# Group 0's output projection in one pass over its weights instead of two

## The chip, the cores and the metric

The kernel runs on one core of a Trainium2 chip. Its engines are TensorE (PE, with its weight loads shown as PEld), VectorE (DVE), ScalarE (ACT), GpSimd (POOL) and SyncE (SP), which issues nearly all of the DMAs. The metric is the device time of one execution in microseconds; lower is better. The time before is 1418.04 us, the median of 3 runs (1415.65 to 1418.85).

## The reference, cut to what matters

One layer of a streaming encoder in fp32, over a group of 1024 new frames and one of 32 frames that continue a stream. The change lies between the three mixers and the feed-forward network:

```
mod = silu(c) @ w_ada + b_ada
sh1, sc1, g1, sh2, sc2, g2 = split(mod, 6)
h = x * (1 + sc1) + sh1
... = split(h @ w_in)                          # mLSTM, forgetting attention, gMLP -> hm, hf, hg
mix = concatenate([hm, hf, hg]) @ w_o           # (tokens, 1024) @ (1024, 1024): the output projection
x = layer_norm(ALPHA * x + (1 + g1) * mix, ln1_g, ln1_b)
h = x * (1 + sc2) + sh2
y = (silu(h @ w_gate) * (h @ w_up)) @ w_down
x = layer_norm(ALPHA * x + (1 + g2) * y, ln2_g, ln2_b)
```

## The kernel before

**Layout.** Activations are kept transposed, features on the partitions: 1024 features are KT = 8 tiles of 128 rows. The 1056 tokens are two groups, c = 0 with 512 tokens and c = 1 with 544, and each group is cut in two halves, `MM[0] = ((0, 256), (256, 512))` and `MM[1] = ((0, 272), (272, 544))`.

**Precision.** A product of fp32 is made of three faster ones. Each operand is split into a rounded high part, cast by ACT, and the rest, subtracted by DVE: of weights by `weights` (L105 and L106, tiles `raw`, `whi`, `wlo`), of the mix by `wo_mix` (L903 and L904, tiles `ah...` and `al...`). `gemm` then issues three matmuls per feature tile, high by high (L117), high by low (L118), low by high (L119). Three tiles of `raw` and three each of `whi` and `wlo` go round.

**Group 0's output projection** is phase `wo` in the trace, at 388.7 to 439.8 us. The mixers left their output in `dmix` in DRAM, and `wo_mix` loads it by 128x256 pieces into four `tmp` buffers, by feature tiles in the order `KORDER = (2, 3, 4, 5, 0, 1, 6, 7)`. For every m, one of eight tiles of output features, `wo` loads 512 KB of w_o, splits it and makes the product, 24 matmuls for a half of the tokens. Before the change `run` calls `wo` once per half:

```
for cut in MM[0]:
    self.wo(0, st, (cut,), nc.vector)
```

so the weights are read and split twice. Group 1's `wo` (phase `wo` at 916.8 to 966 us) has both halves in one call. Only for m = 0 are the products taken feature tile by feature tile over the halves, so that they can follow the mix as it comes.

**What happens to a product.** It lies in one of three PSUM banks (pool `pg`, tiles `wo_g`). `sublayer_end` adds it to the residual z (L943, DVE), which frees the bank, and keeps the sums that the layer norm wants. To keep the squares small, a pivot is taken off z: after m = 0, `ln_pivot` makes the mean of z's first tile with a matmul (L836, tile `wo_t`), ACT copies it to `pv` (L837), and DVE takes it off that tile (L838). For every later m POOL takes it off z (L938) before the product is added. POOL also sums z (L851, `zs`); ACT squares it (L844, L847) and DVE sums the squares (L853, `qs`). Then `ln1` normalises each half and writes it, split again, to the operand of the feed-forward units (`up`), which follow after four units of keys and queries (`fm`).

**What sets the order.** Each engine runs its instructions in one order, laid down ahead of time by a scheduler with a time model of its own; every wait is on the semaphore of an instruction or a DMA. So an instruction that waits holds up whatever stands behind it on its engine, and a load on SP is issued only when those ahead of it are. The profile's line numbers are those of the kernel before; in the changed one the same lines stand 16 further down from `wo` on (L943 becomes L959, L938 becomes L954).

Of the kernel before, what the change touches and what calls it, by code (L numbers as in the profile page):

```python
# [7 lines left out]
F32 = mybir.dt.float32  # L8
F32R = mybir.dt.float32r
AF = mybir.ActivationFunctionType  # L10
ALU = mybir.AluOpType
# [54 lines left out]
def f(ap):  # L66
    return ap.bitcast(F32)


class Kernel:  # L70
# [820 lines left out]
    def operand(self, c, pool):  # L891

        new = lambda tag, n: self.t(pool, [P, KT * 272], F32R, tag, 1)[:, :KT * n].rearrange("p (k n) -> p k n", k=KT)
        self.hh[c], self.hl[c] = ({a: new(f"{x}{a}", b - a) for a, b in MM[c]} for x in ("ah", "al"))

    def wo_mix(self, c, ks):
        self.phase = f"wo{c}"
        nc = self.nc
        for a, b in MM[c]:
            for k in ks:  # L900
                r = self.t(self.p2, [P, 272], F32, "tmp", 4)[:, :b - a]
                self.load(r, self.dmix[c][:, k, a:b])
                nc.scalar.copy(self.hh[c][a][:, k], r)  # L903
                nc.vector.tensor_tensor(self.hl[c][a][:, k], r, f(self.hh[c][a][:, k]), ALU.subtract)  # L904
# [6 lines left out]
    def wo(self, c, st, cuts, eng, res=None):  # L911
# [6 lines left out]
        for m in range(KT):  # L918
# [5 lines left out]
            if m == 0:  # L924
                for i in range(KT):
                    for p, (a, b) in zip(ps, cuts):
                        self.gemm(p[:, :b - a], w[i:i + 1], slice(0, P), lambda _: hh[a][:, ko[i]],
                                  lambda _: hl[a][:, ko[i]], start=i == 0, stop=i == KT - 1)
            for p, (a, b) in zip(ps, cuts):
                if m:  # L930
                    self.gemm(p[:, :b - a], w, slice(0, P), lambda i: hh[a][:, ko[i]], lambda i: hl[a][:, ko[i]])
                self.sublayer_end(c, z, m, p, "g1", st, a, b)
# [19 lines left out]
    def ln1(self, c, st, a, b):  # L952
# [3 lines left out]
        for k in range(KT):  # L956
# [11 lines left out]
            nc.scalar.copy(hh[:, k], h)  # L968
            nc.vector.tensor_tensor(hl[:, k], h, f(hh[:, k]), ALU.subtract)  # L969
# [29 lines left out]
    def up(self, c, j, act, pool, cuts, w=None):  # L999
# [4 lines left out]
        for a, b in cuts:  # L1004
            ps = []
            for i in range(2):
                p = self.t((self.pg, self.pu)[i], [P, 512], F32, self.utag[i])[:, :b - a]
                self.gemm(p, w[i], slice(0, P), lambda k: hh[a][:, k], lambda k: hl[a][:, k])
# [33 lines left out]
    def sup_operand(self, ks):  # L1042
# [164 lines left out]
    def run(self):  # L1207
# [128 lines left out]
        for cut in MM[0]:  # L1336
            self.wo(0, st, (cut,), nc.vector)
# [211 lines left out]
```

## Time and profile before

| | |
|---|---|
| median of 3 runs | 1418.04 us (1415.65 to 1418.85) |
| profiled execution | 1418.36 us, of which the span from first to last instruction is 1416.6 |
| PE busy | 1364.1 us, 96% of the span, in 10945 matmuls |
| DVE, ACT, POOL busy | 1041.1, 657.7 and 255.8 us |
| moved by DMA | 231.97 MB, mean 164 GB/s |
| group 0's output projection | 384 matmuls, from 388.7 to 439.5 us |

A row of a timeline is start, duration, engine, line, operation, tile written, tiles read and shape; in brackets stands how long the engine was idle ahead of it and who ended that. Grouped rows have a count (x24) and durations in nanoseconds. Two matmuls overlap, so one that takes 0.28 us starts 0.12 after the one ahead of it.

### The profile page before, as it was taken

What the parts mean: (1) busy time and instruction counts of PE and PEld (TensorE: products, weight loads), DVE (VectorE), ACT (ScalarE), POOL (GpSimd) and SP (SyncE); (2) the same over time, 40 slices, a digit from 0 to 9 for tenths busy, and PEclk for the clock granted to TensorE, in tenths of its full rate; (3) what the DMA queues carried; (4) which work ended last, traced back from release to release, by engine and by line L of the source; (5) the groups of instructions that cost most, each with busy time, mean ns of one, the idle gap of its engine ahead of it and who ended that gap; (6) DMA issues with size and microseconds to landing.
All of it is one profiled execution on the core that took longest, in us unless ns stands there. A gap on an engine that the chain in (4) does not pass through costs nothing.

```text
span 1416.6 us, 28810 instructions
## 1 busy us (share of the span) xinstructions
PE 1364.1 (96%) x10945; PEld 1312.5 (93%) x10945; DVE 1041.1 (73%) x2363; ACT 657.7 (46%) x1395; POOL 255.8 (18%) x298
## 2 busy tenths in 40 slices
PE   7999999999999899999999999999999999999996
PEld 4799988999889789999999999999999999999996
DVE  5548645678679678687777765678977988878777
ACT  3313234444446464555555453335663454535354
POOL 0103200043157400000000000364610000000331
PEclk9999999999999999999999999999999999999999
DMA  9664578575754765344334422654586567542321
GB/s 359 246 216 132 172 224 238 174 229 157 224 185 147 185 206 173 99 142 148 111 112 146 90 98 86 179 172 128 177 214 182 159 176 202 155 135 92 118 98 64
DMA packets 135698, 231.97 MB, mean 164 GB/s; under 512 B 22516, under 2 KB 79484, under 8 KB 135560
## 3 DMA queue, kind: packets, MB, share of 16 engines
q1 hardware_dynamic: 130520, 220.56, 49.2%
q0 software_dynamic: 4896, 9.44, 4.4%
q8 instruction: 86, 1.41, 0.4%
q14 instruction: 52, 0.43, 0.1%
q10 hardware_dynamic: 144, 0.14, 0.0%
HBM read 196.19 MB, written 52.76 MB: 176 GB/s over the span
## 4 chain that ended last, share of the span: by engine, by line
PE 76%; DVE 9%; DMA 8%; ACT 3%; issue 2%; SPq 1%; POOL 1%; DVEq 0%; ACTq 0%; POOLq 0%
PE up_g L118 6%; PE up_g L119 5%; PE up_g L117 5%; PE dn_g L117 4%; PE dn_g L118 4%; PE dn_g L119 4%; PE tm_g L282 3%; PE tm_g L283 3%; PE tm_g L284 3%; PE fm_g L117 2%; PE fm_g L119 2%; PE fm_g L118 2%; PE fox_t L732 2%; PE wo_g L117 2%; PE wo_g L118 2%
## 5 line engine op out<-in xcount | busy, mean ns | idle before, releaser
L117 PE MATMUL up_g<-wo_ah,up_whi 128*128 128x256 f32 (+1 forms) x720 | 205.4, 286 | 3.9 <-ACT lna_tmp L964 3.3
L118 PE MATMUL up_g<-wo_al,up_whi 128*128 128x256 f32 (+1 forms) x720 | 207.4, 288 | 0.6 <-DVE wo_al L969 0.6
L119 PE MATMUL up_g<-wo_ah,up_wlo 128*128 128x256 f32 (+1 forms) x720 | 205.9, 286 | 0.0
L117 PEld LDWEIGHTS up_g<-wo_ah,up_whi 128*128 128x128 f32 x720 | 136.6, 190 | 5.4 <-ACT wo_ah L968 3.5
L118 PEld LDWEIGHTS up_g<-wo_al,up_whi 128*128 128x128 f32 x720 | 136.8, 190 | 1.6 <-DVE wo_al L969 0.8
L119 PEld LDWEIGHTS up_g<-wo_ah,up_wlo 128*128 128x128 f32 x720 | 136.8, 190 | 0.4 <-DVE up_wlo L106 0.2
L117 PE MATMUL fm_g<-start_h1h,fm_whi 128*128 128x256 f32 (+2 forms) x344 | 102.1, 302 | 8.4 <-DVE fm_qkl L367 3.6
L283 PE MATMUL tm_g<-tm_wlo,start_h1h 128*128 128x256 f32 (+1 forms) x384 | 110.1, 287 | 0.0
L284 PE MATMUL tm_g<-tm_whi,start_h1l 128*128 128x256 f32 (+1 forms) x384 | 109.8, 287 | 0.0
L282 PE MATMUL tm_g<-tm_whi,start_h1h 128*128 128x256 f32 (+1 forms) x384 | 109.2, 286 | 0.2 <-ACT tm_mixs L633 0.2
L117 PE MATMUL dn_g<-up_acth,dn_whi 128*128 128x256 f32 (+1 forms) x352 | 102.4, 291 | 0.2 <-DVE sup_uv L1116 0.2
L118 PE MATMUL fm_g<-start_h1l,fm_whi 128*128 128x256 f32 (+2 forms) x344 | 101.7, 296 | 0.0
L119 PE MATMUL fm_g<-start_h1h,fm_wlo 128*128 128x256 f32 (+2 forms) x344 | 101.1, 295 | 0.0
L118 PE MATMUL dn_g<-up_actl,dn_whi 128*128 128x256 f32 (+1 forms) x352 | 100.5, 286 | 0.0
L119 PE MATMUL dn_g<-up_acth,dn_wlo 128*128 128x256 f32 (+1 forms) x352 | 100.4, 285 | 0.0
L1087 ACT CAST sup_whi<-sup_raw 128x1024 fp32r<-128x1024 f32 x51 | 52.7, 1047 | 80.7 <-PE dn_u L118 28.1
L735 ACT CAST fox_pth<-fox_t 128x256 fp32r<-128x256 f32 (+3 forms) x144 | 51.1, 373 | 67.5 <-PE fox_t L732 63.0
L117 PEld LDWEIGHTS fm_g<-start_h1h,fm_whi 128*128 128x128 f32 x344 | 65.4, 192 | 14.0 <-DVE fm_qkl L367 4.3
L106 DVE TENSOR_TENSOR up_wlo<-up_raw,up_whi 128x1024 fp32r<-128x1024 f32 x52 | 66.2, 1273 | 16.5 <-ACT up_whi L105 15.7
L1088 DVE TENSOR_TENSOR sup_wlo<-sup_raw,sup_whi 128x1024 fp32r<-128x1024 f32 x51 | 63.1, 1244 | 17.0 <-ACT sup_whi L1087 17.0
L105 ACT CAST up_whi<-up_raw 128x1024 fp32r<-128x1024 f32 x52 | 54.5, 1047 | 45.2 <-PE up_g L118 19.7
L736 DVE TENSOR_TENSOR fox_ptl<-fox_t,fox_pth 128x256 fp32r<-128x256 f32 (+3 forms) x144 | 58.0, 417 | 23.7 <-ACT fox_pth L735 22.4
(575 smaller groups left out, 4676.9 us busy)
## 6 DMA issues: line engine op xcount, KB each, us to landing
up_raw<-w_gu SPq DMA_DIRECT2D x52, 512.0 KB
dn_raw<-w_dn SPq DMA_DIRECT2D x28, 512.0 KB
ada_late<-w_ada SPq DMA_DIRECT2D x24, 512.0 KB
wo_raw<-w_o SPq DMA_DIRECT2D x24, 512.0 KB
sup_raw<-w_gu SPq DMA_DIRECT2D x19, 512.0 KB
start_dp<-w_gu SPq DMA_DIRECT2D x18, 512.0 KB
start_dp<-w_gu POOLq DMA_DIRECT2D x18, 512.0 KB, 7.6
sup_raw<-start_dp SPq DMA_DIRECT2D x17, 512.0 KB
```

The costliest lines, as they stand in the source:

```text
L105: nc.scalar.copy(hi[:, :w], raw[:, :w])
L106: (eng or nc.vector).tensor_tensor(lo[:, :w], raw[:, :w], f(hi[:, :w]), ALU.subtract)
L117: nc.tensor.matmul(ps, hi, xh(k), start=start and k == 0, stop=False)
L118: nc.tensor.matmul(ps, hi, xl(k), start=False, stop=False)
L119: nc.tensor.matmul(ps, lo, xh(k), start=False, stop=stop and k == n - 1)
L282: nc.tensor.matmul(ps[:, :ncol], xh, hi, start=k == 0, stop=False)
L283: nc.tensor.matmul(ps[:, :ncol], xh, lo, start=False, stop=False)
L284: nc.tensor.matmul(ps[:, :ncol], xl, hi, start=False, stop=k == 7)
L735: nc.scalar.copy(ph[:, lo:nq], ps[:, lo:nq])
L736: nc.vector.tensor_tensor(pl[:, lo:nq], ps[:, lo:nq], f(ph[:, lo:nq]), ALU.subtract)
L1087: nc.scalar.copy(h, x)
L1088: tt(l, x, f(h), ALU.subtract)
```

## The change

`wo(0, ...)` is called once with both halves, so each unit of w_o is loaded and split once and serves both. The halves' four operand tiles become two of 8 x 544 columns (`ah` and `al`), with the halves as views, and they are allocated once for the projection and the normalised operand after it. `wo_mix` loads whole feature tiles of 128x512 through the two `sil` buffers, 8 loads in place of 16. The later user of this memory, `sup_operand`, takes its four operands as quarters of the two tiles.

```diff
     def operand(self, c, pool):
+        if c == 0:
+            if 0 not in self.hh:
+                tile = lambda tag: self.t(pool, [P, KT * 544], F32R, tag, 1)[:, :KT * 512].rearrange(
+                    "p (k n) -> p k n", k=KT)
+                self.hh[0], self.hl[0] = ({0: x, 256: x[:, :, 256:]} for x in (tile("ah"), tile("al")))
+            return
...
     def wo_mix(self, c, ks):
         self.phase = f"wo{c}"
         nc = self.nc
+        if c == 0:
+            h, l = self.hh[0][0], self.hl[0][0]
+            for k in ks:
+                r = self.t(self.p2, [P, 544], F32, "sil", 2)[:, :512]
+                self.load(r, self.dmix[0][:, k])
+                nc.scalar.copy(h[:, k], r)
+                nc.vector.tensor_tensor(l[:, k], r, f(h[:, k]), ALU.subtract)
+            return
...
         if not self.T:
-            self.T = [[self.t(self.ph, [P, 2176], F32R, f"{x}{i}", 1).rearrange("p (k n) -> p k n", k=4)
-                       for x in ("ah", "al")] for i in (0, 256)]
+            parts = [self.t(self.ph, [P, KT * 544], F32R, x, 1) for x in ("ah", "al")]
+            self.T = [[x[:, i:i + 2176].rearrange("p (k n) -> p k n", k=4) for x in parts] for i in (0, 2176)]
...
         st = self.ln_begin(nc.gpsimd)
-        for cut in MM[0]:
-            self.wo(0, st, (cut,), nc.vector)
+        self.wo(0, st, MM[0], nc.vector)
         self.operand(0, self.ph)
```

The other lines of the diff only cut the operand's views to the width of a half (`hh[:, k]` becomes `hh[:, k, :b - a]`).

On three engines the order around the projection moves. First SP, from the load of feature 6 to the last of the mix. `dmix_31` is group 0's mix, `raw` a unit of w_o, `dqh`, `dql` and `o_kT` are stores of keys and queries. Before:

```order
L87 DMA wo_tmp_5347<-start_dmix_31_87 128x256
L87 DMA wo_tmp_5351<-start_dmix_31_87 128x256
L91 DMA start_dqh_57<-fm_qkh_5336 128x272
L87 DMA wo_tmp_5355<-start_dmix_31_87 128x256
L87 DMA wo_raw_5562<-w_o 128x1024
L91 DMA start_dql_58<-fm_qkl_5337 128x272
L87 DMA wo_tmp_5359<-start_dmix_31_87 128x256
L91 DMA o_kT<-fm_qkr_5338 64x272
```

Here features 6 and 7 of the first half (5347, 5351) stand together, and those of the second half (5355, 5359) behind them. After:

```order
L87 DMA wo_sil_5321<-start_dmix_31_87 128x512
L91 DMA start_dqh_57<-fm_qkh_5310 128x272
L87 DMA wo_raw_5683<-w_o 128x1024
L91 DMA start_dql_58<-fm_qkl_5311 128x272
L87 DMA wo_sil_5325<-start_dmix_31_87 128x512
L91 DMA o_kT<-fm_qkr_5312 64x272
L87 DMA wo_raw_5751<-w_o 128x1024
L87 DMA wo_raw_5819<-w_o 128x1024
```

Two whole tiles stand where four halves stood, and feature 7 (5325) now stands behind a store of queries and the weights of m = 5 (5683), for all 512 tokens.

Second POOL, from the first subtraction of the pivot to the last sum of z. Before:

```order
L938 TENSOR_TENSOR mlstm_z_856_4347<-mlstm_z_856_4347,wo_pv_5376 128x256 x7
L851 TENSOR_TENSOR wo_zs_5374<-mlstm_z_856_4347 128x256
L851 TENSOR_TENSOR wo_zs_5374<-wo_zs_5374,mlstm_z_856_4347 128x256 x6
L938 TENSOR_TENSOR mlstm_z_856_4347<-mlstm_z_856_4347,wo_pv_5376 128x256 x7
L851 TENSOR_TENSOR wo_zs_5374<-mlstm_z_856_4347 128x256
L851 TENSOR_TENSOR wo_zs_5374<-wo_zs_5374,mlstm_z_856_4347 128x256 x6
```

The first three rows are the first half's, the others the second half's. After:

```order
L954 TENSOR_TENSOR mlstm_z_856_4347<-mlstm_z_856_4347,wo_pv_5342 128x256 x7
L851 TENSOR_TENSOR wo_zs_5340<-mlstm_z_856_4347 128x256
L954 TENSOR_TENSOR mlstm_z_856_4347<-mlstm_z_856_4347,wo_pv_5342 128x256 x7
L851 TENSOR_TENSOR wo_zs_5340<-wo_zs_5340,mlstm_z_856_4347 128x256
L851 TENSOR_TENSOR wo_zs_5340<-mlstm_z_856_4347 128x256
L851 TENSOR_TENSOR wo_zs_5340<-wo_zs_5340,mlstm_z_856_4347 128x256 x11
```

The second half's seven subtractions have moved up to right behind the first half's seven and one sum.

Third DVE in the changed kernel, from the last split of the mix on. The products are m0's halves (5349, 5350), m1's (5417, 5418) and m2's first (5485); `wlo` 5550 and 5618 are the weights of m3 and m4:

```order
L911 TENSOR_TENSOR mlstm_al_4357<-wo_sil_5325,mlstm_ah_4356 128x512
L959 SCALAR_TENSOR_TENSOR mlstm_z_856_4347<-wo_g_5349,start_mod_155,mlstm_z_856_4347 128x256
L959 SCALAR_TENSOR_TENSOR mlstm_z_856_4347<-wo_g_5350,start_mod_155,mlstm_z_856_4347 128x256
L106 TENSOR_TENSOR wo_wlo_5550<-wo_raw_5547,wo_whi_5549 128x1024
L838 TENSOR_TENSOR mlstm_z_856_4347<-mlstm_z_856_4347,wo_pv_5342 128x256
L959 SCALAR_TENSOR_TENSOR mlstm_z_856_4347<-wo_g_5417,start_mod_155,mlstm_z_856_4347 128x256
L853 TENSOR_TENSOR wo_qs_5341<-wo_qs_5341,wo_tmp_5445 128x256
L838 TENSOR_TENSOR mlstm_z_856_4347<-mlstm_z_856_4347,wo_pv_5342 128x256
L106 TENSOR_TENSOR wo_wlo_5618<-wo_raw_5615,wo_whi_5617 128x1024
L959 SCALAR_TENSOR_TENSOR mlstm_z_856_4347<-wo_g_5485,start_mod_155,mlstm_z_856_4347 128x256
L959 SCALAR_TENSOR_TENSOR mlstm_z_856_4347<-wo_g_5418,start_mod_155,mlstm_z_856_4347 128x256
```

The addition of m1's second half (5418) stands behind that of m2's first (5485); of the weights only those of m3 and m4 are split in this stretch. Before, m0 to m2 of the first half were added here with the splits of three units, m3 to m5, in a row between them. From the four units of keys and queries on, the order is the same in both programs on every engine.

More of the change, by code (lines that the diff above doesn't have):

```diff
@@ L926, in wo @@
                     for p, (a, b) in zip(ps, cuts):
[L927 to L928 removed]
+                        self.gemm(p[:, :b - a], w[i:i + 1], slice(0, P), lambda _: hh[a][:, ko[i], :b - a],
+                                  lambda _: hl[a][:, ko[i], :b - a], start=i == 0, stop=i == KT - 1)
             for p, (a, b) in zip(ps, cuts):
                 if m:
[L931 removed]
+                    self.gemm(p[:, :b - a], w, slice(0, P), lambda i: hh[a][:, ko[i], :b - a],
+                              lambda i: hl[a][:, ko[i], :b - a])
                 self.sublayer_end(c, z, m, p, "g1", st, a, b)
```

11 lines of the change are left out of this document (6 added, 5 removed).

## The prediction

> **What bounds the kernel now.** I read the page first, then the program cut into four stretches (busy time by window), then what stands ahead of PE's stalls in the stretch that the change touches.
>
> ```profile
> span 1416.6 us, 28810 instructions
> PE 1364.1 (96%) x10945; PEld 1312.5 (93%) x10945; DVE 1041.1 (73%) x2363; ACT 657.7 (46%) x1395; POOL 255.8 (18%) x298
> 388.70:439.80 51.10, 47.70 (x391) 46.86 (x390) 41.63 (x52) 24.86 (x40) 32.30 (x30) 1.00 0.55 186
> 439.80:477.00 37.20, 32.52 (x249) 31.47 (x248) 31.09 (x62) 19.96 (x43) 21.32 (x26) 1.00 0.44 141
> ```
>
> In the window rows the columns after the length are busy PE, weight loads, DVE, ACT, POOL, then the granted clock, the DMA share and GB/s. PE is busy nearly all the span; group 0's output projection is the 51.10 us of the third row. The change leaves every matmul in place, so its worth lies in PE's pauses there, and I need what work alone would take. From PE's timeline:
>
> ```profile
> 388.74 0.28 PE L117 MATMUL wo_g<-mlstm_ah,wo_whi 128*128 128x256 f32 x1
> 397.21 0.29 PE L119 MATMUL wo_g<-mlstm_ah,wo_wlo 128*128 128x256 f32 x1
> 399.33 0.39 PE L117 MATMUL wo_g<-mlstm_ah,wo_whi 128*128 128x256 f32 x1 [1.40 <-ACT wo_whi L105]
> 400.59 0.39 PE L119 MATMUL wo_g<-mlstm_ah,wo_wlo 128*128 128x256 f32 x1 [0.75 <-DVE wo_wlo L106]
> 404.75 0.36 PE L117 MATMUL wo_g<-mlstm_ah,wo_whi 128*128 128x256 f32 x1 [1.25 <-DVE mlstm_z L943]
> L119 PE MATMUL wo_g<-mlstm_ah,wo_wlo x128: 276/281/386, 389.0 to 439.5; 128*128 128x256 f32 x128
> ```
>
> The first two rows are the first and the 72nd matmul: 8.47 us over 71 steps, 0.1193 us each. All 384 need 45.8 us. The last starts at 439.5, so the stage takes 50.9 us and stands still for 5.1, nearly all between 397.2 and 404.8; the bracketed waits (3.40 us) are its visible part. After 405 PE runs without a break: 5.1 us is the most that this stage can give.
>
> **What is removed.** By rows of the whole program and of the stage:
>
> ```profile
> L87 SPq DMA_DIRECT2D wo_raw<-w_o x24: 327/333/1058, 350.5 to 933.5; - x24
> L106 DVE TENSOR_TENSOR wo_wlo<-wo_raw,wo_whi 128x1024 fp32r<-128x1024 f32 x14 | 19.6, 1413 | 4.4 <-ACT wo_whi L105 4.4
> L105 ACT CAST wo_whi<-wo_raw 128x1024 fp32r<-128x1024 f32 x14 | 14.5, 1046 | 13.5 <-PE wo_g L118 5.3 <-issue 3.2 <-DMA wo_raw<-w_o 2.4
> ```
>
> Of 24 weight loads 8 go (one per m of the second pass), with 8 casts of 1.046 us (8.4 us of ACT) and 8 splits of 1.413 us (11.3 us of DVE). Most of that was done after 411, beside saturated PE, and is worth nothing there. The three splits and casts bunched at 398 to 403 are what two of the three waits above name: m3's weights came late. In the new order each unit of weights feeds 48 matmuls (5.7 us), not 24, so weight supply ceases to be a wait. Its price is nothing as long as that cover holds.
>
> **What is moved: the mix.** Now the very first unit needs all eight tiles in full.
>
> ```profile
> L87 SPq DMA_DIRECT2D wo_tmp<-start_dmix x16: 319/382/576, 371.0 to 392.9; - x16
> L903 ACT CAST mlstm_ah<-wo_tmp x16: 395/406/408, 376.8 to 397.9; 128x256 fp32r<-128x256 f32 x16
> L1087 ACT CAST sup_w2h<-sup_raw 128x512 fp32r<-128x512 f32 x17 | 10.4, 611 | 20.4 <-DMA sup_raw<-w_gu 18.6 <-PE sup_u L118 1.8
> L1088 DVE TENSOR_TENSOR sup_w2l<-sup_raw,sup_w2h 128x512 fp32r<-128x512 f32 x17 | 11.6, 685 | 3.4 <-ACT sup_w2h L1087 3.4
> 371.04 5.75 DMA wo_tmp<-start_dmix
> 383.27 2.04 DMA wo_tmp<-start_dmix
> 392.95 4.95 DMA wo_tmp<-start_dmix
> ```
>
> Sixteen half loads become eight whole ones; 512-wide casts and splits of other tiles cost 0.611 and 0.685 us. Against two casts of 0.406 each, ACT gains 8 × 0.2 = 1.6 us beside the waits for landing, so nothing. From issue to landing the chain of waits shows 2.04 to 5.75 us. The last half (392.95, landing 397.90) held up ACT and so m3's weights, but PE did not need its data until the second pass; the last whole tile is needed at once. When is it issued? SP is in order, and its row stands behind m5's weights, which wait for m2's split, and its buffer waits for feature 1's split:
>
> ```profile
> 389.90 1.23 DVE L106 TENSOR_TENSOR wo_wlo<-wo_raw,wo_whi 128x1024 fp32r<-128x1024 f32 x1 [1.44 <-ACT wo_whi L105]
> 391.04 0.50 DVE L367 SCALAR_TENSOR_TENSOR fm_qkl<-fm_g,start_qsc,fm_qkh 128x272 fp32r<-128x272 f32 x1
> 391.98 0.40 SPq L87 DMA_DIRECT2D wo_raw<-w_o  x1
> ```
>
> m2's split still ends at 391.13, since it waits for PE's previous product. The next small DVE row ends at about 391.5, feature 1's split (0.685) at 392.2, and SP issues the last tile at 392.25. Behind it on SP stand only a key store and later weights, which nobody needs for 10 us. As before a 512 KB weight load lies a microsecond ahead of it; the half tile that was also ahead is gone and this tile is twice the size, so I take the 4.95 us of before, less 0.05: it lands at 397.15 and is cast by T = 397.8. The bounds are 2.04 and 5.75 us, from 394.3 to 398.0, and by bytes 2 × 4.95 = 9.9.
>
> In the Trainium skill, "DMA: Bandwidth & Descriptors" (section Anatomy of one DMA) gives about 2.0 us fixed plus bytes over 436 GB/s, for loads issued by POOL; an estimate from it for 256 KB is 2.6 us, and PE would hardly wait for this tile: the no-pause rival below. The row of 4.95 us for half the size disagrees, as that load queued behind others.
>
> **PE from T on.** Ahead of the last tile PE has 7/8 of 48 matmuls and of the 24 of m1's first half: 63, done at 388.74 + 63 × 0.1193 = 396.25. It pauses 1.6 us to T, does three matmuls, waits for the split (T + 0.74) and does six: T + 1.45. The product of m0's first half ends some 0.2 sooner; its addition to z (0.473 us, row L943 below) frees the bank that m1's second half needs, and with the pivot's matmul that starts at T + 2.15. Three products and two pivots later (8.6 + 0.25) PE is ready for m3 at T + 11.0.
>
> **The new wait on POOL.** m3's first product needs the bank of m1's second half, and that addition to z waits for POOL's subtraction of the second half's pivot, now queued behind all seven of the first half and a sum.
>
> ```profile
> L943 DVE SCALAR_TENSOR_TENSOR mlstm_z<-wo_g,start_mod,mlstm_z 128x256 f32<-128x256 f32 x16 | 7.4, 473 | 0.2 <-POOL mlstm_z L938 0.2
> 401.52 7.44 POOL L938 TENSOR_TENSOR mlstm_z<-mlstm_z,wo_pv 128x256 f32<-128x256 f32 x7 [8.75 <-ACT wo_pv L837]
> 408.93 0.92 POOL L851 TENSOR_TENSOR wo_zs<-mlstm_z 128x256 f32<-128x256 f32 x1
> L938 POOL TENSOR_TENSOR mlstm_z<-mlstm_z,wo_pv x14: 741/922/1737, 401.5 to 429.8; 128x256 f32<-128x256 f32 x14
> 926.66 5.76 POOL L938 TENSOR_TENSOR wo_z<-wo_z,wo_pv 128x272 f32<-128x272 f32 x7 [18.46 <-ACT wo_pv L837]
> 934.92 0.63 DVE L943 SCALAR_TENSOR_TENSOR wo_z<-wo_g,start_mod,wo_z 128x240 f32<-128x240 f32 x2 [1.00 <-POOL wo_z L938]
> ```
>
> ACT copies the pivot after m3's cast (1.046), which waits for m0 to end: T + 1.45 + 0.1 + 1.05 + 0.37 puts POOL's start at T + 2.95. Group 1 already runs this order: from 926.66 to the freed addition at 934.92 is 8.26 us. So the addition ends at T + 11.7 and m3 starts at T + 11.8: 0.8 us late. By group 0's own rows nine operations take 7.44 + 0.92 + 1.06 = 9.4 us (T + 12.9); by the shortest, 9 × 0.741 = 6.7, nobody waits (T + 11.0). I take group 1's, being the same queue. Behind the waiting addition on DVE stand m2's sums and additions and m5's split, needed at T + 17 or later; ACT's square and m5's cast wait with them, with the same slack.
>
> A rule that speaks to this: "SBUF — State Buffer" of the Trainium skill (section Who interferes with whom) says a DVE instruction with two SBUF inputs and a POOL instruction that reads SBUF exclude one another for a whole instruction. The shortest row (0.741) beside the mean of 1.06 in a stretch full of splits agrees; with fewer splits that rule would put the queue nearer the short end.
>
> **The sum.** Ten products remain: 239 steps, 28.5 us, last start T + 40.3 = 438.1 against 439.5: 1.4 us gained. Before the stage one stall may shrink, since fewer loads let SP issue its small load sooner:
>
> ```profile
> 378.45 0.63 PE L649 MATMUL tm_g<-tm_gvn,start_wsp 32*32 32x64 f32 x8 [1.03 <-DMA tm_gvn<-start_dvn]
> ```
>
> The bytes queued ahead of it stay; of 0 to 1.03 us I take 0.3. After the stage both programs run the same order on every engine, so the rest shifts whole, at no cost; the operand tile that normalisation rewrites is free once the last product has read it, as the old one was. Total −1.7 us. The profiled execution took 1418.36 us (span 1416.6 and 1.76 around it), 0.32 above the median of 1418.04: 1416.7 on its own scale, **1416.3** on the median's.
>
> **Rivals.** 0.2% (2.8 us) is about what a measurement of this kernel can tell from no change.
>
> *No pause at all*, as in group 1:
>
> ```profile
> L117 PE MATMUL wo_g<-up_ah,wo_whi x128: 282/287/322, 916.9 to 965.6; 128*128 128x272 f32 x128
> ```
>
> 384 matmuls in 48.9 us, with no bracketed wait on PE. If the last tile lands by 395.6 (3.3 us) and POOL keeps the short rate, the 5.1 us go but for the pivots' 0.5: −4.6 − 0.3, 1413.1. Against it: there the mix had been loaded beside earlier work. Chance 0.20.
>
> *The clock.* After the stage PE stands still and then runs slow (PE timeline and windows):
>
> ```profile
> 476.86 0.36 PE L117 MATMUL up_g<-wo_ah,up_whi 128*128 128x256 f32 x1 [3.33 <-ACT lna_tmp L964]
> 478.00:479.00 1.00, 1.00 (x6) 0.88 (x6) 0.93 (x4) 1.00 (x4) 1.00 (x1) 0.59 0.81 280
> 479.00:480.00 1.00, 1.00 (x7) 1.00 (x7) 0.84 (x2) 1.00 (x3) 1.00 (x3) 0.50 0.63 235
> 480.00:481.00 1.00, 1.00 (x6) 1.00 (x6) 0.47 (x1) 1.00 (x4) 1.00 (x3) 0.50 0.00 1
> 481.00:482.00 1.00, 1.00 (x9) 1.00 (x8) 0.93 (x3) 0.96 (x4) 1.00 (x3) 0.71 0.48 102
> ```
>
> The four clocks fall short of 1 by 0.41 + 0.50 + 0.50 + 0.29 = 1.7 us. If the shifted stall does not trip that drop, −1.7 − 1.7: 1414.6. "TensorE: Matmul & The Clock Gate" (Part 1: The HAM clock gate) of the Trainium skill has a free-running window of about 3.4 us that must be idle for the drop, so a stall of 3.3 can go either way. The shorter stalls at 399 left the clock at 1.00. Chance 0.10.
>
> *The whole tile comes too late*: slower. If its time goes with its bytes (9.9 us), it lands at 402.15, T is 402.8, and the last start 443.1: +3.6 − 0.3, 1421.3. It decides from a landing of 398.5 us on, a latency of 6.3, beyond every one seen. For: two buffers of whole tiles, and nothing else to do for PE. Chance 0.15.
>
> **Chances and range.** The forecast has 0.55, mostly inside 0.2%: 0.08 of it lies beyond on the fast side (a tile at 396, the small load's full 1.0), 0.01 on the slow side (the queue's 9.4 with a late tile). Faster: 0.08 + 0.20 + 0.10 = 0.38. Slower: 0.11 of the late tile and 0.01: 0.12. Same: 0.50. The range reaches from just below the no-pause case, 1412.9, to most of the late tile, 1420.6.
>
> **What would show it.** Right: the bracket ahead of the third matmul group names the last tile's cast, about 1.6 us near 396 to 398; the next is the addition to z behind L954 on POOL, about 0.8; the last L119 starts near 438; weights name no wait. Wrong: a last tile landing outside 395.6 to 398.5, a POOL queue far from 8.3 us, or a stretch after the stage whose length differs by over 1 us.

## The result, and the profile after

| | before | after |
|---|---|---|
| median, us (lowest to highest; 14 runs each) | 1417.74 (1413.73 to 1418.85) | 1415.20 (1409.07 to 1421.22) |
| ratio to before, 95% interval | | 0.9990, 0.9974 to 1.0006 |
| profiled execution, us (span) | 1418.36 (1416.6) | 1421.22 (1419.4) |

The change made no difference that these runs can tell from zero: 2.5 us less by the medians, from 3.7 less to 0.9 more by the interval. A second timing, further below, gave 0.9975 (0.9958 to 0.9992), a gain of a quarter of a percent. The profiled execution of the changed kernel is the slowest of its 14 runs, so where its time lies has to be read stage by stage.

The stage by busy time, from its first product to the end of its last one, in the changed kernel (columns as in the prediction: length, PE, weight loads, DVE, ACT, POOL, granted clock, DMA share, GB/s):

```profile
span 1419.4 us, 28721 instructions
390.57:442.82 52.25, 49.37 (x392) 48.50 (x391) 30.20 (x42) 16.98 (x30) 26.75 (x30) 0.97 0.36 117
```

Before, DVE was busy 41.63 us and ACT 24.86 in about this stretch. The work that the change removes is gone, yet the stage is longer, and its clock is 0.97 instead of 1.00. PE's timeline shows the products with a wait, and the first and the last:

```profile
390.57 0.28 PE L117 MATMUL wo_g<-mlstm_ah,wo_whi 128*128 128x256 f32 x1
394.66 0.62 PE L117 MATMUL wo_g<-mlstm_ah,wo_whi 128*128 128x256 f32 x3 [0.38 <-ACT mlstm_ah L910]
401.26 0.62 PE L117 MATMUL wo_g<-mlstm_ah,wo_whi 128*128 128x256 f32 x3 [2.40 <-ACT mlstm_ah L910]
442.54 0.28 PE L119 MATMUL wo_g<-mlstm_ah,wo_wlo 128*128 128x256 f32 x1
```

From first to last start the stage takes 51.97 us against 50.76 before. No wait names weights any more, and none names the addition to z; one pause for the last tile of the mix has taken the place of all three. ACT's and SP's rows show how that tile came (L910 is the cast of a mix tile, `wo_sil` its buffer):

```profile
388.32 0.38 SPq L87 DMA_DIRECT2D wo_sil<-start_dmix  x1
393.99 0.62 ACT L910 CAST mlstm_ah<-wo_sil 128x512 fp32r<-128x512 f32 x1 [1.91 <-DMA wo_sil<-start_dmix]
395.42 0.32 SPq L87 DMA_DIRECT2D wo_sil<-start_dmix  x1
400.59 0.62 ACT L910 CAST mlstm_ah<-wo_sil 128x512 fp32r<-128x512 f32 x1 [4.15 <-DMA wo_sil<-start_dmix]
```

Feature 1's tile, issued at 388.32, is cast 5.67 us later; its split ends at 395.39 and frees the buffer in which the last tile is issued, 4.85 us after the first product, to be cast 5.17 us after that. And then the clock drops (windows of PE's clock, same columns):

```profile
401.00:402.00 1.00, 0.64 (x4) 0.43 (x4) 0.69 (x1) 0.21 (x1) 0.00 (x0) 1.00 0.00 0
402.00:403.00 1.00, 1.00 (x6) 1.00 (x6) 0.47 (x2) 0.26 (x1) 0.00 (x0) 0.68 0.00 0
403.00:404.00 1.00, 1.00 (x5) 0.89 (x4) 0.62 (x3) 0.79 (x1) 0.00 (x0) 0.50 0.00 0
404.00:405.00 1.00, 1.00 (x6) 0.91 (x5) 1.00 (x2) 0.37 (x1) 0.22 (x1) 0.50 0.00 0
405.00:406.00 1.00, 1.00 (x7) 1.00 (x7) 1.00 (x3) 0.05 (x1) 1.00 (x2) 0.61 0.00 0
```

0.32 + 0.50 + 0.50 + 0.39 = 1.71 us are lost. The 2.8 us by which this span is longer add up as follows. Before the stage, in identical code up to 366 us, the changed kernel runs 2.13 us late; from there to the first product it takes 22.32 us instead of 22.62 (0.30 gained); the stage costs 1.21; the rest, 976.9 against 977.1 us, gains 0.2. The 2.13 us are no work of the change: every engine runs the same instructions in the same order up to there, and a second trace of the kernel before came to that point at 368.55 us, later than this one (368.25). Part of it is the clock: this trace has two drops, at 245 and 310 us, that the first trace of before has not.

### The profile page after: what moved, and what is told of

Read it like the earlier page. It is cut to its first block, busy times and chain, and to the rows that moved or that the text cites. A ratio compares the mean times of both kernels' runs of the same rounds, so it can differ in the third digit from the quotient of the medians.

```text
span 1419.4 us, 28721 instructions
## 1 busy us (share of the span) xinstructions
PE 1368.3 (96%) x10945; PEld 1315.4 (93%) x10945; DVE 1028.8 (72%) x2347; ACT 649.0 (46%) x1379; POOL 250.1 (18%) x298
## 3 DMA queue, kind: packets, MB, share of 16 engines
q0 software_dynamic: 4896, 9.44, 4.5%
## 4 chain that ended last, share of the span: by engine, by line
PE 76%; DVE 8%; DMA 8%; ACT 3%; issue 2%; POOL 1%; SPq 1%; DVEq 0%; ACTq 0%; POOLq 0%
PE up_g L118 5%; PE up_g L119 5%; PE up_g L117 5%; PE dn_g L117 4%; PE dn_g L118 4%; PE dn_g L119 4%; PE tm_g L282 3%; PE tm_g L283 3%; PE tm_g L284 3%; PE fox_t L732 2%; PE wo_g L118 2%; PE sup_u L117 2%; PE wo_g L119 2%; PE sup_u L118 2%; PE sup_u L119 2%
## 5 line engine op out<-in xcount | busy, mean ns | idle before, releaser
L117 PE MATMUL up_g<-mlstm_ah,up_whi 128*128 128x256 f32 x656 | 187.0, 286 | 4.3 <-ACT lna_tmp L980 3.3
L118 PE MATMUL up_g<-mlstm_al,up_whi 128*128 128x256 f32 x656 | 188.8, 288 | 0.6 <-DVE mlstm_al L985 0.6
L119 PE MATMUL up_g<-mlstm_ah,up_wlo 128*128 128x256 f32 x656 | 187.3, 286 | 0.0
L117 PEld LDWEIGHTS up_g<-mlstm_ah,up_whi 128*128 128x128 f32 x656 | 124.5, 190 | 5.8 <-ACT mlstm_ah L984 3.4
L118 PEld LDWEIGHTS up_g<-mlstm_al,up_whi 128*128 128x128 f32 x656 | 124.8, 190 | 1.5 <-DVE mlstm_al L985 0.8
L119 PEld LDWEIGHTS up_g<-mlstm_ah,up_wlo 128*128 128x128 f32 x656 | 124.9, 191 | 0.4 <-DVE up_wlo L106 0.2
L282 PE MATMUL tm_g<-tm_whi,start_h1h 128*128 128x256 f32 (+1 forms) x384 | 110.4, 289 | 0.2 <-ACT tm_mixs L633 0.2
L282 PEld LDWEIGHTS tm_g<-tm_whi,start_h1h 128*128 128x128 f32 x384 | 73.5, 192 | 2.6 <-issue 1.6
```

The costliest lines, as they stand in the source:

```text
L117: nc.tensor.matmul(ps, hi, xh(k), start=start and k == 0, stop=False)
L118: nc.tensor.matmul(ps, hi, xl(k), start=False, stop=False)
L119: nc.tensor.matmul(ps, lo, xh(k), start=False, stop=stop and k == n - 1)
L282: nc.tensor.matmul(ps[:, :ncol], xh, hi, start=k == 0, stop=False)
```

## The experiments

**What every trace gave.** The stage is first to last start as above. "Cast" is when ACT begins to cast the last piece of the mix, counted from the first product. "Lead" runs from PE's first L282 product that waits for tm_mixs (366.12 us in the trace of before) to the stage's first product, in code that all of them share but for where the mix's loads and casts stand. Ratios are to the kernel before on the same chip.

| kernel | lead | cast | PE's waits in the stage | drop in it | stage | ratio (95%) |
|---|---|---|---|---|---|---|
| before | 22.62 | | 1.40, 0.75, 1.25 | no | 50.76 | |
| before, again | 22.27 | | 0.81, 0.75, 1.26 | no | 50.23 | |
| after | 22.32 | 10.02 | 0.38, 2.40 | yes | 51.97 | 0.9990 (0.9974 to 1.0006) |
| after, again | 21.89 | 11.21 | 0.65, 3.08 | yes | 53.14 | |
| after, timed | 22.33 | 8.75 | 1.11 | no | 49.47 | 0.9975 (0.9958 to 0.9992) |
| halves | 21.51 | 9.44 | 0.21, 0.99 | no | 48.54 | 0.9970 (0.9954 to 0.9985) |
| two passes | 22.38 | 8.34 | 1.34, 0.62 | yes | 51.49 | 0.9995 (0.9974 to 1.0016) |
| warm | 22.44 | 8.38 | none | no | 48.86 | 0.9999 (0.9983 to 1.0014) |
| in place | 25.54 | before it | none | no | 46.60 | 0.9979 (0.9964 to 0.9994) |
| z late | 24.19 | 3.32 | none | no | 46.76 | 0.9978 (0.9959 to 0.9997) |
| in place, z late | 26.32 | before it | none | no | 46.38 | 0.9995 (0.9982 to 1.0008) |
| pivot on DVE | 22.28 | 8.70 | 1.69 | yes | 50.68 | |
| evacuation first | 22.79 | before it | none | no | 46.39 | 0.9969 (0.9949 to 0.9989) |
| weights behind | 21.51 | 5.98 | 0.18 | no | 47.14 | 0.9966 (0.9947 to 0.9985) |

**One part of the change alone.** The halves keep the single pass and bring the mix by half tiles; two passes keep the whole tiles and undo the single pass.

```diff
 halves, in wo_mix for c == 0:
+            for a, b in MM[0]:
                 for k in ks:
-                r = self.t(self.p2, [P, 544], F32, "sil", 2)[:, :512]
+                    r = self.t(self.p2, [P, 272], F32, "tmp", 4)[:, :256]
...
 two passes:
-        self.wo(0, st, MM[0], nc.vector)
+        for cut in MM[0]:
+            self.wo(0, st, (cut,), nc.vector)
```

> One pass over the weights as in the changed kernel, but the mix comes by half tiles through four buffers of 272, as before. Theory A (the stage's length is set by when the last piece of the mix is cast, and weights are no longer a wait): the last half tile is cast about 9.5 us after the stage's first product instead of 10.6, PE has 69 products to do before it instead of 63, so its pause shrinks from 2.40 to 0.6 to 1.4 us, the granted clock stays at 1.00, and the stage takes 49 to 50.3 us instead of 52.0. Rival D (fewer and larger loads, casts and splits are themselves worth something): the stage is no shorter than 52.0. Rival C (the queue of subtractions on POOL sets the end): a wait ahead of the third unit of about 0.8 us or more appears, and the stage stays above 51.

> Whole tiles of the mix as in the changed kernel, but two passes over the weights, one for each half of the tokens, as before. Theory A: the pause for the last whole tile stays at about 2.4 us with the same drop of the clock (1.7 us), and one or two waits for weights are added to it (together 0.5 to 2 us), stage 52 to 54.5 us, time 1416 to 1419. Rival D (the number of loads and casts matters, the pass order doesn't): stage as in the kernel before or shorter, 50.8 or less. Rival C (POOL's queue): the queue goes back to that of before, with the subtraction first served when it is needed, so the stage falls to about 51.

The halves bore theory A out: the last half is cast at 9.44, about as expected, PE has more to do before it, the pause is 0.99 and the clock stays. The stage, 48.54, is a little below the range, and this kernel is measurably faster than before. Fewer and larger loads (rival D) earned nothing by themselves. With two passes and whole tiles the pause was smaller than expected (1.34, as the tile came at 8.34) but the clock dropped after it, and the stage is longer than in either trace of before. (Its time, 1413.3, is below the range expected, but so was that of the kernel before in that comparison, 1413.7.) Rival C's figure, a stage of about 51, is as near to 51.5 as theory A's; whether POOL's queue sets the stage is tested below. By the stages, then, the single pass is worth something and the whole tiles cost something, and together they nearly cancel. The times bear out the first half only: two passes with whole tiles took as long as the kernel before (0.9995, 0.9974 to 1.0016), and the intervals of the halves and of the changed kernel overlap, so the cost of the whole tiles rests on the stages.

**The clock.** Twelve extra products ahead of the second unit's first half, which overwrites them, so that PE has work in the pause.

```diff
+                if c == 0 and m == 1 and a == 0:
+                    for _ in range(12):
+                        nc.tensor.matmul(p[:, :b - a], w[0][0], hh[a][:, ko[0], :b - a], start=True, stop=True)
                 if m:
                     self.gemm(p[:, :b - a], w, slice(0, P), lambda i: hh[a][:, ko[i], :b - a],
```

> The changed kernel with twelve extra products (1.43 us) into the bank of the second unit's first half, ahead of its own first one, which overwrites them: they run on PE before the last tile of the mix has come and nothing waits for them. Theory B (the pause of 2.40 us trips the clock, and that costs 1.7 us of clock): the pause shrinks to about 1.0 us, the granted clock stays at 1.00 through 400 to 412, and the stage falls by 0.8 to 1.7 us (0.8 if the third unit then waits for the addition behind POOL's queue, which the slow clock hides now), though PE does 1.43 us more work. Rival (the slow clock comes from something else, or costs nothing): the clock falls as before and the stage stays at 52.0 or grows.

With 1.43 us more work the stage was 3.1 us shorter, and the clock stayed. That is more than expected, because the last tile also came 1.64 us earlier here; a cleaner pair is the changed kernel's third trace and the next experiment, with equal casts (8.75 and 8.70): 49.47 without a drop and 50.68 with one, 1.2 us apart. (That is 0.5 less than the 1.71 us of clock that a drop takes; why is not shown.) The total did not fall with the stage (0.9999); no whole-kernel gain was shown.

**POOL's queue.** One subtraction moved from the end of POOL's queue to DVE.

```diff
+        eng = self.nc.vector if c == 0 and m == 1 and a and self.phase == "wo0" else self.nc.gpsimd
-        less = lambda: self.nc.gpsimd.tensor_tensor(z[:, m, sl], z[:, m, sl], st["pv"][:, sl], ALU.subtract)
+        less = lambda: eng.tensor_tensor(z[:, m, sl], z[:, m, sl], st["pv"][:, sl], ALU.subtract)
```

> The changed kernel with one subtraction of the pivot (second half of the second unit) done on DVE instead of at the end of the first half's queue on POOL. Rival C of the queue (the third unit waits for it): the third unit starts up to 0.8 us earlier and the stage falls by as much. Theory A (that queue ends when PE is ready in any case): the stage's length from the last tile's cast on changes by less than 0.3 us. The clock: by the grid of 3.41 us that all traces so far show (a drop follows a stretch of the grid in which PE was busy for less than about half), a pause of about 2.4 us trips it in some three runs of four; so a stage of 52 us with the drop at 402 to 406, or of about 50.5 without.

From the last tile's first product (395.58) to the last start (436.89) this took 41.31 us, against 442.54 − 401.26 = 41.28 in the changed kernel; both had the drop. The queue on POOL costs PE nothing. The changed kernel's own rows, POOL's queue and then DVE's addition behind it:

```profile
404.78 6.64 POOL L954 TENSOR_TENSOR mlstm_z<-mlstm_z,wo_pv 128x256 f32<-128x256 f32 x7 [9.32 <-ACT wo_pv L837]
411.39 0.74 POOL L851 TENSOR_TENSOR wo_zs<-mlstm_z 128x256 f32<-128x256 f32 x1
412.86 0.48 DVE L959 SCALAR_TENSOR_TENSOR mlstm_z<-wo_g,start_mod,mlstm_z 128x256 f32<-128x256 f32 x1 [1.15 <-POOL mlstm_z L954]
```

DVE does wait, 1.15 us; PE doesn't. In both of these kernels the slow clock could hide a short wait, so the changed kernel's third trace, without a drop, is the better witness:

```profile
409.21 0.28 PE L117 MATMUL wo_g<-mlstm_ah,wo_whi 128*128 128x256 f32 x1
409.35 0.48 DVE L959 SCALAR_TENSOR_TENSOR mlstm_z<-wo_g,start_mod,mlstm_z 128x256 f32<-128x256 f32 x1 [2.22 <-POOL mlstm_z L954]
```

The first row is the stage's 145th product, the first of m3. It starts 0.12 us after the one ahead of it, before the addition has begun.

**Making the mix early.** Three ways to take the late tile away: no buffers (the load goes into the tile of the low parts, which is cast and split in place); z's 2 MB behind the mix; both.

```diff
 in place:
-                r = self.t(self.p2, [P, 544], F32, "sil", 2)[:, :512]
+                r = f(l[:, k])
 z late:
-        self.wo_res(0, self.pz)
         self.operand(0, self.ph)
         self.wo_mix(0, self.KORDER[:6])
...
         self.wo_mix(0, self.KORDER[6:])
+        self.wo_res(0, self.pz)
```

> The changed kernel with the mix loaded straight into the tile of its low parts, cast from there and split in place: no buffers to wait for, so all eight whole loads can be issued at once, about 20 us ahead of the last one now. Theory A: no pause for the mix and no drop of the clock; a wait of about 0.8 us for the addition behind POOL's queue may show in their place; stage 47 to 48.3 us instead of 52.0. Against that, the small load that PE waits for near 380 now stands behind six whole tiles: by 1.5 MB at 312 GB/s 5 us, which puts it 0 to 3 us later. In all 1411 to 1414. Rival C (POOL's queue sets the end of the stage): no more than 1.7 us shorter, 50.3 or more. Rival (what is gained in the stage is lost ahead of it): the stage shrinks and the wait near 380 grows by as much.

> The changed kernel with one edit: the eight loads of the residual tile z (2 MB), which stand ahead of the mix on SP's queue, are asked for behind the mix in the program. The mix keeps its two buffers of whole tiles. Theory A (the last tile is late because the chain of loads through two buffers starts late, behind 2 MB): the first pair of tiles is cast 4 to 5 us earlier, each later pair with it, the last tile is cast before PE has run out of products, and the pause and the drop of the clock go: stage 46.8 to 48.5 us instead of 52.0, time 1409 to 1412. Rival (the last tile is late because of its own latency of 5.1 us at its place in SP's queue, whatever was ahead): it is cast at the same 10 to 10.6 us after the first product, the pause stays, stage 50 to 52. Rival (the 2 MB only move, and press on the small load near 380 or the weights): a wait of 1 to 3 us appears there.

> The mix loaded straight into the tile of its low parts, as in the experiment in place, and the loads of z behind the mix as well. In the experiment in place PE stood still 2.35 us near 378 because ACT, in order, waited in a cast for a tile of the mix that landed late, behind 2 MB of z, and lost 1.7 us to a drop of the clock after it. Theory: with z behind the mix the tiles land about 5 us earlier, the casts no longer hold up ACT, the wait near 380 falls to 0.5 or less and the clock stays; the stage keeps its 46.6 us. Time 1407 to 1409.5. Rival (the small load for that place, behind six whole tiles, is what holds): the wait stays at 1.5 to 2.5 us and names that load; time 1411 to 1413.

All three ended the pause, as theory A had it, with a stage of 46.4 to 46.8 us (in the first 0.4 below its range), and lost 1.9 to 4.0 us of it in the lead (against the changed kernel's 22.32), each with a drop of the clock there. So in the first the rival that expects the gain to be lost ahead was right in part (3.2 of 5.4 us), and in the second the one that expected a wait near 380 (1.57 us at 376.5), though it names the copy and not the small load. For the third the theory fell: the wait grew instead of going. ACT is in order, and its rows show why, here in the kernel in place, with PE's wait behind them:

```profile
376.57 1.26 ACT L910 CAST mlstm_ah<-mlstm_al 128x512 fp32r<-128x512 f32 x2 [2.51 <-DMA mlstm_al<-start_dmix]
378.34 0.62 ACT L910 CAST mlstm_ah<-mlstm_al 128x512 fp32r<-128x512 f32 x1 [0.51 <-DMA mlstm_al<-start_dmix]
378.87 0.48 ACT L366 ACTIVATE fm_qkh<-fm_g,start_qsc 128x272 fp32r<-128x272 f32 x1
379.25 0.36 ACT L633 COPY tm_mixs<-tm_g 128x256 f32<-128x256 f32 x1
379.67 0.39 PE L117 MATMUL fm_g<-start_h1h,fm_whi 128*128 128x272 f32 x1 [2.35 <-ACT tm_mixs L633]
```

and in the kernel in place with z late, where the casts stand further ahead on ACT and hold up an evacuation and the weights of the unit before:

```profile
371.49 0.62 ACT L910 CAST mlstm_ah<-mlstm_al 128x512 fp32r<-128x512 f32 x1 [3.47 <-DMA mlstm_al<-start_dmix]
373.26 0.62 ACT L910 CAST mlstm_ah<-mlstm_al 128x512 fp32r<-128x512 f32 x1 [1.16 <-DMA mlstm_al<-start_dmix]
373.79 0.36 ACT L644 COPY tm_traw<-tm_g 128x256 f32<-128x256 f32 x1
374.57 1.05 ACT L105 CAST fm_whi<-fm_raw 128x1024 fp32r<-128x1024 f32 x1
377.92 0.60 PE L117 MATMUL fm_g<-start_h1h,fm_whi 128*128 128x272 f32 x1 [2.61 <-ACT tm_mixs L633]
```

**The casts out of the way.** If ACT's order is the cause, putting the casts behind that copy must cure it.

```diff
 in place, with wo_mix(c, ks, step): 0 loads only, 1 casts and splits only
-        self.wo_mix(0, self.KORDER[:6])
+        self.wo_mix(0, self.KORDER[:6], 0)
...
+        with tc.issue_after(self.mixcopy[-2].ins):      # the copy of tm_mixs for the last full tile
+            self.wo_mix(0, self.KORDER[:6], 1)
         for h in range(QD, PRE):
```

> The experiment in place with one thing more: the loads of the mix stay where they are, but its casts on ACT are put behind the copy that evacuates the last full tile of the units before (tm_mixs), so that ACT does not sit in a cast for a tile that has not landed while PE waits for that copy. Theory: the stage keeps its 46.6 us, the wait of 2.35 us near 378 falls to 1.0 or less (the 0.87 that every trace shows before it included), the clock stays through 370 to 440, and the time is 1407 to 1409.5. Rival (the small load behind six whole tiles holds PE as well): a wait of 1 to 3 us that names tm_gvn or the evacuation behind it; time 1410 to 1412, no better than the halves.

It did: 46.39 us, no drop between 252 and 473 us, and a kernel that is faster than before (by 0.3%, 0.1 to 0.5%). In its rows (one line further down, L634) the copy now goes first and the casts wait for nothing that PE needs:

```profile
380.12 0.36 ACT L634 COPY tm_mixs<-tm_g 128x256 f32<-128x256 f32 x1
380.37 2.19 ACT L913 CAST mlstm_ah<-mlstm_al 128x512 fp32r<-128x512 f32 x4
380.53 0.39 PE L117 MATMUL fm_g<-start_h1h,fm_whi 128*128 128x272 f32 x1 [0.62 <-ACT tm_mixs L634]
```

The median, 1411.3, lies above the 1409.5 expected and in the rival's range; that was 5.2 below the 1416.5 of the kernel before in that comparison, and the rival's wait of 1 to 3 us is not there.

**The same kernels once more.** Was the first trace of the changed kernel an odd draw?

> The changed kernel once more, for a second trace of the same order of instructions. In three traces with the same mix loads the last whole tile was issued 4.2 us after the stage's first product and its cast began at 8.3 to 8.7; in the first trace of the changed kernel at 4.85 and 10.0. Theory (the first trace was a late draw of the landing): issue near 4.2, cast at 8.3 to 9, pause 1.2 to 1.8 us. Rival (the order of the changed kernel makes it late): 4.85 and 10 again, pause 2.4. The clock: with a pause of 1.7 a drop follows in about six executions of ten, by the grid; without it the stage takes about 49 us, with it about 50.7.

> The kernel before once more. Its stage has pauses of 1.40, 0.75 and 1.25 us within 7.5 us, and the clock stayed at 1.00 in the trace shown. Theory (a drop follows where a stretch of the run's own grid of 3.41 us has PE busy for less than about half): at four to six positions of the grid in ten a stretch of this pattern is that empty, so the drop can show here as well, and then costs 1.7 us: stage 50.8 or 52.5. Rival (only a single pause of about 2 us or more trips it): clock 1.00 again, stage 50.8.

The first theory fell: the second trace was later still, 11.21 us and a pause of 3.08. The other one is undecided; before's pauses were shorter this time (2.82 us in all) and left the clock alone, which both readings allow.

**What makes the last tiles late.** The weights' loads among them put behind the last one.

```diff
+            with ExitStack() as es:
+                if c == 0 and m == 4:
+                    es.enter_context(self.tc.issue_after(self.mixload.ins))     # the last mix load
-            w = self.weights(self.d["w_o"][m], KT, P, eng)
+                w = self.weights(self.d["w_o"][m], KT, P, eng)
```

> The changed kernel with one edit: the loads of the weights of the fifth unit and, in SP's order behind it, of the sixth (512 KB each) are put behind the last tile of the mix; in the changed kernel they stand among the last three or four tiles. PE needs these weights some 20 us later. Theory (the last tiles land late because 1 MB of weights is moved with them): the last four tiles land after 3.0 to 4.2 us each instead of 4.1 to 6.1, the last tile's cast begins 6 to 8 us after the stage's first product instead of 8.3 to 11.2, the pause is 1.2 us or less, mostly without a drop of the clock; stage 48 to 49.5 us, time 1410 to 1413. Rival (a whole tile takes 4 to 6 us by itself, from this memory to this tile): landing and pause stay, stage 50.5 to 53.

> The changed kernel itself, timed beside the run above and the kernel before on the same chip, with a third trace. Two traces of it had the last tile's cast at 10.0 and 11.2 us after the stage's first product, pauses of 2.40 and 3.08 us and a drop of the clock in both; three traces of kernels with the same loads had 8.3 to 8.7. Theory (the landing varies from execution to execution): 8.3 to 11.2 again, pause 1.3 to 3.1, stage 49 to 53, time within 0.3% of the kernel before. Rival (the changed kernel's own order makes it always late): cast at 10 or later, pause 2.4 or more.

With the weights behind, feature 1's tile is cast 2.97 us after its issue and the last tile about 3.9 after its own:

```profile
385.43 0.32 SPq L87 DMA_DIRECT2D wo_sil<-start_dmix  x1
388.40 0.62 ACT L910 CAST mlstm_ah<-wo_sil 128x512 fp32r<-128x512 f32 x1 [1.55 <-DMA wo_sil<-start_dmix]
389.01 1.09 SPq L87 DMA_DIRECT2D wo_sil<-start_dmix  x2
390.15 0.42 SPq L87 DMA_DIRECT2D wo_raw<-w_o  x1
392.98 1.30 ACT L910 CAST mlstm_ah<-wo_sil 128x512 fp32r<-128x512 f32 x2 [2.62 <-DMA wo_sil<-start_dmix]
```

(Rows with x2 hold two instructions; the second load starts at 389.78, and the second cast is done at 394.28.) In the six other traces with these loads of the mix those two latencies were 5.0 to 5.7 and 4.1 to 6.1 us. The pause is 0.18, the stage 47.14, 0.9 under the range, the lead 0.8 shorter than the changed kernel's, and the kernel is faster than before by 0.3% (0.15 to 0.5%), as good as the one with the evacuation first. Against the changed kernel beside it the medians are 1411.39 and 1414.51 us, but the two intervals overlap, so the time alone doesn't show the gain over the changed kernel. That kernel's third trace came early, at 8.75: its landing varies by 2.5 us from trace to trace, as the theory of that run had it. The second and third traces are of different chips, so what is the execution's and what the chip's isn't told apart.

## Why the prediction was right, and where it wasn't

**Right.** The time, 1416.3, is 1.1 above the median measured, and the reason holds: the weights cease to be a wait, and the last whole tile takes their place. The rest shifted whole (976.9 against 977.1 us; 974.5 to 977.1 over the five traces of the two kernels). In the third trace the stage is the one forecast, with one pause for the last tile (1.11 against 1.6):

```profile
397.89 0.62 PE L117 MATMUL wo_g<-mlstm_ah,wo_whi 128*128 128x256 f32 x3 [1.11 <-ACT mlstm_ah L910]
```

Its stage is 1.29 us shorter than before, against 1.4 forecast.

**Luck in it.** That agreement is partly errors that offset one another: PE was done with what precedes the last tile 8.15 us after the first product and not 7.5, after small waits; the tile was cast 0.3 later; and m3 began at T + 11.4 (T is the end of the last cast) with no wait on POOL, where the sum had T + 11.0 and 0.8 of waiting. The other two traces are not the forecast's: the last tile's cast began 10.0 and 11.2 us after the first product, where the prediction named a landing outside 6.9 to 9.8 (395.6 to 398.5) as the sign of being wrong, and their stages were longer than before. The lead gained 0.30 us, as taken, but before's second trace had 22.27, so this size isn't shown: the stall that was to shrink did, from 1.03 and 0.82 us to 0.36 or less, and a wait of about 0.4 for tm_mixs came right behind it.

**The last tile's issue was mis-sized.** The sum let feature 1's split end with the splits of before and put the issue 3.5 us after the first product. It was 4.2 to 5.1, since feature 1's tile, itself a whole one behind 512 KB of weights, is cast 5.0 to 5.7 us after its issue; with the weights behind it takes 2.97. The step counted the queue for the last tile and not for the one whose buffer it needs. The changed kernel's last cast began at 8.75 to 11.21; the forecast had the tile land at 8.4. The latency of the last tile itself, 4.9 in the forecast, was 4.5 to 6.1 to the cast.

**The clock was left out of this pause.** The forecast reasoned that the stalls at 399 had left the clock at 1.00 and weighed only the stall at 477. Two of three traces of the changed kernel lost 1.71 us of clock after the new pause. In the first (51.97) that is what makes the stage longer than before (50.76) instead of about equal or a little shorter; in the second (53.14) the late tile would have done it alone.

**The wait on POOL did not come.** The queue was right (404.78 to 412.86 is 8.08 us, forecast 8.26), its start and end 0.4 to 0.7 late (T + 3.6 and T + 12.1, T = 401.2 being the end of the last cast), but no trace shows PE wait for it. The step that failed is that m3's first product needs the bank of m1's second half. In the third trace that product starts at 409.21, before the addition of m1's second half (409.35 to 409.83), so it has another bank. DVE adds m2's first half ahead, so that bank is free earlier (407.12); that m3 takes this one is inferred, the traces don't name banks. For "SBUF — State Buffer" of the Trainium skill (section Who interferes with whom), by which fewer splits should shorten POOL's queue: seven subtractions took 6.64 us (7.03 in the third trace) against 7.44 before, a tenth less at most. The number of splits isn't it, since the halves, with two beside the queue as in the changed kernel, took 7.52. Over all traces it goes with the time that DVE spends in instructions with two tensor inputs meanwhile: beside 3.0 to 4.6 us of them the seven took 5.9 to 6.7 us, beside 5.1 to 6.4 us 7.0 to 7.5. That agrees with the rule; no run varies it alone.

**The rivals.** The whole tile too late, which the prediction has decide from 9.8 us after the first product on, happened in the first two traces of three (10.02 and 11.21; stages 1.2 and 2.4 us longer than before), by a later issue more than by a latency beyond the 6.3 it asked for (5.2 and 6.1 to the cast). No pause at all is what the experiments with an early mix reach, 46.4 us, 4.4 below before against the 4.6 it was given.

**Open.** Three traces of the changed kernel average 51.5 us in the stage, two of before 50.5, while 26 timed runs say 0.1 to 0.25% faster. Its runs spread over 12 us, and two of the three profiled ones, at 1421.2 and 1420.0, stand at the top of that spread; so the traces may have drawn late tiles more often, but that isn't shown. Nor is why the landing varies.

## What to carry to other kernels

When a change makes PE need data sooner, work out the arrival of that data along its whole chain: the buffer it reuses, the load before it in that buffer, and what stands ahead of each on the queue. Loading earlier helps only if the in-order engine that consumes the load has nothing urgent behind that step: three experiments bought 5 us in the stage and paid 2 to 4 of them back ahead of it, where ACT's queue held PE and the clock dropped after it, while two loads of weights moved behind the mix gave as much as the best of the larger edits. And price a pause of PE with its clock, for the chance that it trips.

## What the runs showed of the hardware

The drops of the clock lie on a grid. In the changed kernel's trace they start at 142.96, 245.36, 310.20, 402.36, 480.88, 876.82, 1173.78 and 1245.46 us (from windows of 1 us: a window of 0.68 holds 0.64 us at half clock). All distances are whole multiples of 3.4133 within 0.02 us, for example 92.16 = 27 × 3.413, and each drop lasts 3.41 us, or twice that, and costs 1.71 us of clock for each 3.41. (One more, at 1412.7 on the same grid, lasts to the end of the program.) Every one of the 14 traces has such a grid, with a phase of its own. How full the stretch of the grid just ahead was goes with whether a drop comes. In the changed kernel, in the one of two passes, and in the changed kernel's third trace, each with its next stretch:

```profile
398.95:402.36 3.41, 0.99 (x6) 0.79 (x7) 0.69 (x1) 0.62 (x1) 0.00 (x0) 1.00 0.03 7
402.36:405.78 3.42, 3.42 (x16) 3.22 (x15) 2.87 (x4) 1.42 (x2) 1.00 (x2) 0.50 0.00 0
```

```profile
395.21:398.62 3.41, 1.97 (x13) 1.41 (x11) 1.07 (x2) 1.11 (x2) 0.00 (x0) 1.00 0.09 32
398.62:402.03 3.41, 3.24 (x12) 2.72 (x12) 2.93 (x4) 2.71 (x4) 0.62 (x1) 0.50 0.14 36
```

```profile
396.97:400.38 3.41, 2.28 (x13) 1.82 (x14) 1.59 (x4) 1.66 (x2) 0.00 (x0) 1.00 0.00 0
400.38:403.80 3.42, 3.42 (x30) 3.37 (x29) 2.93 (x4) 1.58 (x5) 2.91 (x4) 1.00 0.34 114
```

Cutting all 14 traces (from 138 us on, without the last 20 us or so) along their own grids, and counting the stretches at full clock by PE's busy time and by whether a drop follows:

| PE busy in the 3.41 us | stretches | followed by a drop |
|---|---|---|
| under 1.5 | 56 | 56 |
| 1.5 to 2.1 | 30 | 11 |
| 2.1 to 3.0 | 114 | 0 |
| over 3.0 | 4724 | 0 |
| any, from 860 to 890 us | 105 | 17 |

In the last row PE shows no pause and drops follow all the same. The changed kernel's stretch there, and some of its products:

```profile
873.40:876.82 3.42, 3.42 (x36) 2.75 (x35) 1.41 (x4) 0.52 (x2) 0.00 (x0) 1.00 0.48 153
875.77 0.30 PE L820 MATMUL foxs_o<-foxs_pth,start_vs 32*64 32x32 f32 x2
876.00 0.42 PE L820 MATMUL foxs_o<-foxs_pth,foxs_v 128*64 128x32 f32 x4
```

These products have 32 columns (the last figure of the shape), and PE counts as busy all through. Counted by columns, the row falls in two: the 17 stretches ahead of a drop hold at most 2564, the other 88 at least 2690, where a full stretch of products of 256 columns holds about 7300 (3.41 / 0.1193 × 256). Over all traces a drop followed 62 of 64 stretches under 2560 columns, 21 of 53 from there to 3500, and 1 of some 4900 above. So what counts is nearer to the columns than to PE's busy time, and no bound is sharp. (The last 20 us, which both counts leave out, have stretches as empty without a drop behind them, two of them with PE busy for 1.43 and 1.46 us.)

"TensorE: Matmul & The Clock Gate" of the Trainium skill (Part 1: The HAM clock gate) gives a free-running window of 3413 ns, and the traces agree to the digit; it has the drop after an idle window, where here a window with PE busy for up to 1.5 us, or with a third of its columns, was enough. A pause of 1.3 us can therefore cost up to 1.7 more in one execution and nothing in the next. That makes a kernel with pauses spread without any change in its instructions: in the changed kernel's 14 runs the clock lost from 11.3 to 19.9 us of the span (span times 1 less the mean granted clock), and by and large the longer runs are those that lost more (correlation 0.8). It is not the whole of the spread. The 2.13 us by which the changed kernel's first trace ran late ahead of the change go with two more drops (3.4 us), but its third trace had the same drops there and came to that point at 366.15, as early as the kernel before.
